# Turning tokens into features: 32x32 transposes on VectorE in place of 128x128 ones on TensorE, in one decoder block

## The chip, the cores and the metric

The kernel runs on one core of a Trainium2 chip. The metric is the device time of one execution in microseconds; where several executions were made, the median stands for them. A separate, profiled execution gives the trace; its own time is given beside its span.

## What is computed

One layer of a hybrid decoder on 256 tokens of 2048 features, all in fp32:

```python
h = rmsnorm(x, norm_mix_g)
c_g, b_g, xa, za, q, fl, iv, og, ga, gb = split(h @ w_in)
ya = b_g * causal_dwconv3(c_g * xa, conv_w) * silu(za)
# log_f and kk come from sigmoid(fl), sigmoid(-fl)
o = hgrn2_chunked(silu(q), kk, iv, log_f)          # gated linear recurrence, 8 heads of 128
yb = rmsnorm_per_head(o) * hg_norm_g * silu(og)
m = sigmoid(ga) * (ya @ w_a_out) + sigmoid(gb) * (yb @ w_b_out)
x = x + m @ w_o
x = x + sigmoid(rmsnorm(x, ple_norm_g) @ w_ple_gate) * (p @ w_ple_proj)
out = rmsnorm(x, final_norm_g)
```

Every product has the activations' features on the contracted axis. A product leaves tokens on the partitions (two tiles of 128 tokens) and 512 features along the free axis; whatever goes into a further product, into the convolution along the tokens or into the recurrence must have features on the partitions. So blocks of 256 tokens x 512 features are turned from tokens to features: one *turn* in the sense of this text.

## The kernel before

**Groups and steps.** The work is a list of groups, each one block of 512 output columns: for column block j = 0 and 1 the groups f, q, iv, og, c, xa, za, b; then for j = 0 to 3 the groups ga, gb, A (ya times w_a), B (yb times w_b); then four groups O (m times w_o); then PP and PG for each of four blocks. A group is cut into steps along the contracted axis, 256 features each: eight steps for most groups, four for A and B, one for PP. In this text steps are counted from zero over the whole kernel: f is 0 to 7, q 8 to 15, iv 16 to 23, og 24 to 31, c 32 to 39, xa 40 to 47, za 48 to 55, b 56 to 63, and then the same for j = 1.

**A step.** The weights arrive in fp32 by one SP queue into `raw` (three buffers, two steps each). For precision each weight block is split in two parts: ScalarE writes the high part `whi` (L118) and VectorE the rest `wlo` = raw - whi (L119). Activations are split the same way by `put` (L154 and L155). TensorE then does twelve matmuls for a step: two blocks of 128 features, two token tiles, and three products each, high by high (L805), high activations by `wlo` (L806), low activations by `whi` (L807). Splits are written three steps ahead of use, and there are four buffers of each part, so `whi` of step n+3 can be written when TensorE has finished step n-1.

**Epilogues.** When a group's last step is written, a generator for it is started; after each later step, `advance()` runs every active generator up to its next `yield`. So the work behind a group is spread over the following steps, between the splits. The written order is what the framework starts from; it then draws up the order on each engine, and an instruction that is ready early may go ahead of others.

**The turns.** Before, `transposed` (L170 to L184) does eight 128x128 transposes on TensorE against an identity, into two banks of the PSUM tag `s`, and a reader takes the result from PSUM. `ep_o` has the same in its own lines (L576). The eighteen turns are:

- f (two): L218, read by four sigmoids on ScalarE (L223, L224). A chain of scalings, logarithms (L244) and a scan (L253) follows.
- q (two): L270, copied to SBUF by VectorE (L274).
- yb, the output of the recurrence (two): L456, read by `put`.
- xa (two): L474, read by the convolution, four heads of one L487 and seven L493 on VectorE.
- b (two): L512, multiplied with the convolution on VectorE (L517), then split (L520, L521).
- B (four): L551, split on ScalarE and VectorE (L556, L557) into `mT`.
- O (four): L576, read by `put` into `x1T`.

Beside them in the same steps runs `hgrn`, the recurrence (L292 to L461), started after og: level by level differences and products on VectorE and GpSimd (L355, L338), small products on TensorE (L310), masked copies on VectorE (L314), a reciprocal (L400), and at its end a sum of squares (L443) and eight products (L450) that make yb. The tail of xa's convolution and the middle of `hgrn` meet in steps 48 to 58, and b's turn and the end of `hgrn` meet in steps 64 to 69.

Scratch tiles come from `t4`, eight buffers of 128x1024 in the first part and five in the later ones.

Of the kernel before, what the change touches and what calls it, by code (L numbers as in the profile page):

```python
# [9 lines left out]

F32 = mybir.dt.float32
F32R = mybir.dt.float32r
AF = mybir.ActivationFunctionType
ALU = mybir.AluOpType
# [31 lines left out]
def hybrid_kernel(ctx, tc, xT, x, pT, prm, gfin, masks, w_in, w_a, w_b, w_o, w_pg, w_pp, out):  # L46
# [35 lines left out]
    def bank(tag):  # L82
        return ps.tile([P, CW], F32, tag=tag, bufs=4, name=nm(tag))
# [39 lines left out]

    prm_t = const.tile([P, PRM_N], F32, name="prm_t")
    nc.scalar.dma_start(out=prm_t, in_=prm)
    ident = const.tile([P, P], F32, name="ident")
    make_identity(nc, ident)

    if PAD_CONST:
        nc.gpsimd.memset(const.tile([P, PAD_CONST], F32, name="pad"), 0.0)  # L130
# [36 lines left out]
        nc.gpsimd.tensor_tensor(out=r, in0=v, in1=mhalf[:, :n], op=ALU.pow)  # L167
        return r

    def transposed(src):  # L170

        banks = []
        for half in range(2):
            b = bank("s")
            for i in range(2):
                c = half * 2 + i
                for t in range(NT):
                    nc.tensor.transpose(  # L178
                        b[:, i * T + t * P : i * T + (t + 1) * P],
                        src[:, t * CW + c * P : t * CW + (c + 1) * P],  # L180
                        ident,
                    )
            banks.append(b)
        return banks  # L184


    def scaled(psum, dst):
# [26 lines left out]
    def ep_f(j, psum):  # L214
        fl = t4()
        scaled(psum, fl)
        yield
        bk = transposed(fl)  # L218
        yield
        sg, sn = t4(), t4()  # L220
        for h in range(2):
            s = slice(h * 512, (h + 1) * 512)
            nc.scalar.activation(out=sg[:, s], in_=bk[h], func=AF.Sigmoid)  # L223
            nc.scalar.activation(out=sn[:, s], in_=bk[h], func=AF.Sigmoid, scale=-1.0)  # L224
        yield
        kT = t4("kT", 1)
        for h in range(4):
            s = slice(h * T, (h + 1) * T)
            hd = j * 4 + h
            nc.vector.tensor_scalar(  # L230
                out=sg[:, s], in0=sg[:, s], scalar1=state["oml"][:, hd : hd + 1],
                scalar2=state["lbm"][:, hd : hd + 1], op0=ALU.mult, op1=ALU.add,
            )
            nc.vector.tensor_scalar(
                out=kT[:, s], in0=sn[:, s], scalar1=state["oml"][:, hd : hd + 1], scalar2=None,
                op0=ALU.mult,
            )
        yield


        lf, last = t4(), sc(8, "lfl", 2)
        lv, fv = segments(lf), segments(sg)
        nc.gpsimd.memset(lv[:, :, 1, :, 0:1], 0.0)
        nc.scalar.activation(out=lv[:, :, 0], in_=fv[:, :, 0], func=AF.Ln)  # L244
        nc.scalar.activation(
            out=lv[:, :, 1, :, 1:], in_=fv[:, :, 1, :, : SCAN - 1], func=AF.Ln
        )
        nc.scalar.activation(
            out=last.rearrange("p (h s) -> p h s", h=4), in_=fv[:, :, 1, :, SCAN - 1], func=AF.Ln
        )  # L250
        yield
        b, tot = t4("b", 1), sc(16, "tot", 2)
        nc.vector.tensor_tensor_scan(  # L253
            out=b, data0=carry, data1=lf, initial=0.0, op0=ALU.mult, op1=ALU.add
        )
        bv, tv = segments(b), tot.rearrange("p (h k s) -> p h k s", h=4, k=2)
        nc.vector.tensor_copy(out=tv[:, :, 0], in_=bv[:, :, 0, :, SCAN - 1])
        nc.vector.tensor_tensor(
            out=tv[:, :, 1], in0=bv[:, :, 1, :, SCAN - 1],
            in1=last.rearrange("p (h s) -> p h s", h=4), op=ALU.add,  # L260
        )
        state["kT", j], state["b", j], state["tot", j] = kT, b, tot

    def ep_q(j, psum):
        sg, qt = t4(), t4()
        sig(psum, sg)
        times(psum, sg, qt)
        yield
        yield
        bk = transposed(qt)  # L270
        yield
        qT = t4("qT", 1)
        for h in range(2):
            nc.vector.tensor_copy(out=qT[:, h * 512 : (h + 1) * 512], in_=bk[h])  # L274
        state["qT", j] = qT

    def ep_iv(j, psum):
# [14 lines left out]
    def hgrn(j):  # L292
# [159 lines left out]
                op0=ALU.mult, op1=ALU.mult,  # L452
            )
        yield
        yield
        bk = transposed(yb)  # L456
        yield
        for h in range(2):
            for i in range(2):
                k = j * 4 + h * 2 + i  # L460
                put(state["ybT"], k, bk[h][:, i * T : (i + 1) * T], gain(PRM_GHG, k))  # L461

    def ep_c(j, psum):
        c = t4()
# [4 lines left out]
    def ep_xa(j, psum):  # L469
        cx = t4()  # L470
        times(psum, state["c", j], cx)
        yield
        yield
        bk = transposed(cx)  # L474
        yield
        cv = t4("cv", 1)
        for h in range(2):
            for i in range(2):
                n = h * 2 + i
                k = j * 4 + n  # L480
                d, s = cv[:, n * T : (n + 1) * T], bk[h][:, i * T : (i + 1) * T]

                def w(tap):
                    c = PRM_CONV + tap * 8 + k
                    return prm_t[:, c : c + 1]

                nc.vector.tensor_scalar(out=d, in0=s, scalar1=w(2), scalar2=None, op0=ALU.mult)  # L487

                for tap, to, fr, n_ in (
                    (1, 1, 0, P - 1), (1, P, P + 1, P - 1), (1, T - 1, P - 1, 1),  # L490
                    (0, 2, 0, P - 2), (0, P, P + 2, P - 2), (0, T - 2, P - 1, 1), (0, T - 1, P - 2, 1),
                ):
                    nc.vector.scalar_tensor_tensor(  # L493
                        out=d[:, to : to + n_], in0=s[:, fr : fr + n_], scalar=w(tap), in1=d[:, to : to + n_],
                        op0=ALU.mult, op1=ALU.add,
                    )
            yield
        state["cv", j] = cv
# [8 lines left out]
    def ep_b(j, psum):  # L507
        bz = t4()
        times(psum, state["zs", j], bz)
        yield  # L510
        yield
        bk = transposed(bz)  # L512
        yield
        ya = t4()
        for h in range(2):
            s = slice(h * 512, (h + 1) * 512)
            nc.vector.tensor_tensor(out=ya[:, s], in0=state["cv", j][:, s], in1=bk[h], op=ALU.mult)  # L517
        yield
        hi, lo = (x[:, j * 4 : (j + 1) * 4, :].rearrange("p k t -> p (k t)") for x in state["yaT"])
        nc.scalar.activation(out=hi, in_=ya, func=AF.Copy)  # L520
        nc.vector.tensor_tensor(out=lo, in0=ya, in1=hi.bitcast(F32), op=ALU.subtract)  # L521
# [21 lines left out]
    def ep_bb(j, psum):  # L543
        ga, gb = state["ga", j], state["gb", j]
        for t in range(NT):
            s = slice(t * CW, (t + 1) * CW)
            nc.vector.tensor_tensor(out=gb[:, s], in0=gb[:, s], in1=psum[t], op=ALU.mult)  # L547
        nc.gpsimd.tensor_tensor(out=gb, in0=ga, in1=gb, op=ALU.add)  # L548
        yield
        yield  # L550
        bk = transposed(gb)  # L551
        yield
        for h in range(2):
            k = j * 4 + h * 2
            hi, lo = (x[:, k : k + 2, :].rearrange("p k t -> p (k t)") for x in state["mT"])
            nc.scalar.activation(out=hi, in_=bk[h], func=AF.Copy)  # L556
            nc.vector.tensor_tensor(out=lo, in0=bk[h], in1=hi.bitcast(F32), op=ALU.subtract)  # L557

    def ep_o(j, psum):
        xs = state["x"]  # L560
        src = t4()
        for t in range(NT):
            d = xs[:, t, j * CW : (j + 1) * CW]
            nc.vector.tensor_tensor(out=d, in0=d, in1=psum[t], op=ALU.add)
            nc.scalar.activation(
                out=src[:, t * CW : (t + 1) * CW], in_=d, func=AF.Square,
                accum_out=state["ss2"][:, t * 4 + j : t * 4 + j + 1],
            )
        yield
        bk = []  # L570
        for half in range(2):
            b = bank("s")
            for i in range(2):
                c = j * 4 + half * 2 + i
                for t in range(NT):
                    nc.tensor.transpose(  # L576
                        b[:, i * T + t * P : i * T + (t + 1) * P], xs[:, t, c * P : (c + 1) * P], ident
                    )
            bk.append(b)
        yield  # L580
        for h in range(2):
            for i in range(2):
                k = j * 4 + h * 2 + i
                put(state["x1T"], k, bk[h][:, i * T : (i + 1) * T], gain(PRM_GPLE, k))
        if j == 3:
            tot = sc(2, "tot2", 1)
            nc.vector.tensor_reduce(
                out=tot, in_=state["ss2"].rearrange("p (t j) -> p t j", t=NT),
                axis=mybir.AxisListType.X, op=ALU.add,
            )  # L590
            state["rstd2"] = rsqrt_of(tot, NT, D, "r2")
# [369 lines left out]
```

## Time and profile before

| | us |
|---|---|
| median of three executions | 852.69 (852.5 to 853.07) |
| the profiled execution's own time | 852.66 |
| its span | 850.9 |
| TensorE's eight-transpose groups, L178 and L576, durations summed | 10.6 + 4.1 + 4.1 |
| wlo L119 on VectorE, all | 372.6 |
| whi L118 on ScalarE, all | 308.6 |

The profile lists each engine's busy time, the chain of work that ended last (followed back from the last instruction through what released each step), groups of instructions by source line with the mean duration of one, the waits between engines, and a timeline. In the names, PE is TensorE, PEld its weight load, DVE is VectorE, ACT is ScalarE, POOL is GpSimd, and SP the queue that issues transfers. Matmuls are pipelined, so a row's duration is longer than the distance to the next row, and it is the distance that adds up. In the waits, "A <- B" means that A stood idle until B released it; the three numbers are the total, the count and the longest, in us. In the rows of groups, the numbers behind the bar are busy us in all, mean ns of one, and the idle time just before. A bracket in the timeline gives the idle time before that row and what ended it; a row without one began at once. TensorE's granted clock is 0.998 of full speed over the span.

### The profile page before, as it was taken

What the parts mean: (1) busy time and instruction counts of PE and PEld (TensorE: products, weight loads), DVE (VectorE), ACT (ScalarE), POOL (GpSimd) and SP (SyncE); (2) the same over time, 40 slices, a digit from 0 to 9 for tenths busy, and PEclk for the clock granted to TensorE, in tenths of its full rate; (3) what the DMA queues carried; (4) which work ended last, traced back from release to release, by engine and by line L of the source; (5) the groups of instructions that cost most, each with busy time, mean ns of one, the idle gap of its engine ahead of it and who ended that gap; (6) DMA issues with size and microseconds to landing.
All of it is one profiled execution on the core that took longest, in us unless ns stands there. A gap on an engine that the chain in (4) does not pass through costs nothing.

```text
span 850.9 us, 9907 instructions
## 1 busy us (share of the span) xinstructions
PE 839.6 (99%) x3897; PEld 697.8 (82%) x3897; DVE 527.2 (62%) x611; ACT 425.0 (50%) x514; POOL 82.8 (10%) x76
## 2 busy tenths in 40 slices
PE   9999999999999999999999999999999999999995
PEld 6788888888888888888888888888888888888885
DVE  7484686977674587968446446446446555556572
ACT  7854664434644754534443444444444554455553
POOL 1010042202010042101001001001001000001110
PEclk9999999999999999999999999999999999999999
DMA  9865464444555455444555555555555955554542
GB/s 340 335 215 184 158 223 162 171 174 155 191 199 177 169 198 178 169 165 174 169 191 191 198 197 199 171 193 188 190 198 173 362 181 186 184 196 165 197 149 99
DMA packets 25966, 164.12 MB, mean 193 GB/s; under 512 B 3008, under 2 KB 3008, under 8 KB 7744
## 3 DMA queue, kind: packets, MB, share of 16 engines
q1 hardware_dynamic: 25488, 162.93, 53.8%
q8 instruction: 30, 0.49, 0.2%
q10 hardware_dynamic: 432, 0.56, 0.2%
q14 instruction: 16, 0.13, 0.0%
HBM read 161.39 MB, written 2.10 MB: 192 GB/s over the span
## 4 chain that ended last, share of the span: by engine, by line
PE 96%; issue 1%; DMA 1%; ACT 1%; DVE 0%; SPq 0%; POOLq 0%; POOL 0%; ACTq 0%
PE g L806 31%; PE g L807 31%; PE g L805 31%; PE s L310 1%; PE s L178 1%; DMA raw<-in_w_in 1%; PE s L418 0%; PE s L576 0%; PE s L430 0%; PE s L431 0%; PE s L429 0%; ACT whi L118 0%; ACT xs L647 0%; ACT t L630 0%; SPq L700 0%
## 5 line engine op out<-in xcount | busy, mean ns | idle before, releaser
L119 DVE TENSOR_TENSOR wlo<-raw,whi 128x1024 fp32r<-128x1024 f32 (+1 forms) x294 | 372.6, 1273 | 270.6 <-ACT whi L118 270.0
L118 ACT ACTIVATE whi<-raw 128x1024 fp32r<-128x1024 f32 (+1 forms) x294 | 308.6, 1053 | 361.9 <-PE g L807 354.4
L805 PE MATMUL g<-whi,xh 128*128 128x512 f32 (+1 forms) x912 | 354.5, 389 | 0.9 <-ACT whi L118 0.9
L806 PE MATMUL g<-wlo,xh 128*128 128x512 f32 (+1 forms) x912 | 352.0, 386 | 0.2 <-DVE wlo L119 0.2
L807 PE MATMUL g<-whi,xl 128*128 128x512 f32 (+1 forms) x912 | 351.8, 386 | 0.0
L805 PEld LDWEIGHTS g<-whi,xh 128*128 128x128 f32 x912 | 171.5, 188 | 35.5 <-ACT whi L118 2.3
L806 PEld LDWEIGHTS g<-wlo,xh 128*128 128x128 f32 x912 | 171.5, 188 | 34.8 <-DVE wlo L119 1.2
L807 PEld LDWEIGHTS g<-whi,xl 128*128 128x128 f32 x912 | 171.4, 188 | 34.4
L805 PE MATMUL g<-whi,mh 128*128 128x512 f32 x128 | 50.2, 392 | 0.0
L807 PE MATMUL g<-whi,ml 128*128 128x512 f32 x128 | 49.9, 390 | 0.0
L806 PE MATMUL g<-wlo,mh 128*128 128x512 f32 x128 | 49.8, 389 | 0.0
L548 POOL TENSOR_TENSOR gb<-ga,gb 128x1024 f32<-128x1024 f32 x4 | 9.6, 2396 | 258.3 <-DVE gb L547 258.3
L807 PEld LDWEIGHTS g<-whi,ml 128*128 128x128 f32 x128 | 24.0, 188 | 5.1
L806 PEld LDWEIGHTS g<-wlo,mh 128*128 128x128 f32 x128 | 24.0, 188 | 4.9
L805 PEld LDWEIGHTS g<-whi,mh 128*128 128x128 f32 x128 | 24.0, 188 | 4.8
L338 POOL TENSOR_TENSOR X<-t,kT 128x256 f32<-128x256 f32 x12 | 11.5, 956 | 168.3 <-ACT t L352 115.4
L805 PE MATMUL g<-whi,yaTh 128*128 128x512 f32 x64 | 24.9, 389 | 0.0
L806 PE MATMUL g<-wlo,yaTh 128*128 128x512 f32 x64 | 24.9, 389 | 0.0
L807 PE MATMUL g<-whi,yaTl 128*128 128x512 f32 x64 | 24.9, 389 | 0.0
L805 PE MATMUL g<-whi,ybTh 128*128 128x512 f32 x64 | 24.9, 389 | 0.0
L806 PE MATMUL g<-wlo,ybTh 128*128 128x512 f32 x64 | 24.9, 389 | 0.0
L807 PE MATMUL g<-whi,ybTl 128*128 128x512 f32 x64 | 24.9, 389 | 0.0
(153 smaller groups left out, 559.1 us busy)
## 6 DMA issues: line engine op xcount, KB each, us to landing
raw<-in_w_in SPq DMA_DIRECT2D x91, 1024.0 KB, 4.8
raw<-in_w_o SPq DMA_DIRECT2D x16, 1024.0 KB, 4.8
raw<-in_w_pg SPq DMA_DIRECT2D x16, 1024.0 KB, 4.7
raw<-in_w_a SPq DMA_DIRECT2D x8, 1024.0 KB, 5.0
raw<-in_w_b SPq DMA_DIRECT2D x8, 1024.0 KB, 5.0
raw<-in_w_in SPq DMA_DIRECT2D x9, 512.0 KB, 7.8
t<-in_xT SPq DMA_DIRECT2D x8, 256.0 KB, 7.0
t<-in_x SPq DMA_DIRECT2D x4, 512.0 KB, 8.7
```

The source lines that it names most:

```text
L118: nc.scalar.activation(out=hi[:, s], in_=src[:, s], func=AF.Copy)
L119: nc.vector.tensor_tensor(out=lo[:, s], in0=src[:, s], in1=hi[:, s].bitcast(F32), op=ALU.subtract)
L178: nc.tensor.transpose(b[:, i * T + t * P : i * T + (t + 1) * P], src[:, t * CW + c * P : t * CW + (c + 1) * P], ident,)
L310: nc.tensor.matmul(bk[:, s], X[:, 0, h, :], X[:, 1, h, :], start=True, stop=True)
L338: eng.tensor_tensor(out=xv[:, w, :, :, half, :], in0=ev[:, :, blk, :, half, :], in1=src[:, :, blk, :, half, :], op=ALU.mult,)
L548: nc.gpsimd.tensor_tensor(out=gb, in0=ga, in1=gb, op=ALU.add)
L805: nc.tensor.matmul(psum, oh, hi, start=first, stop=False)
L806: nc.tensor.matmul(psum, oh, lo, start=False, stop=False)
L807: nc.tensor.matmul(psum, ol, hi, start=False, stop=last)
```

## The change

All eighteen turns move to VectorE. `transposed`, its TensorE transposes and the identity go. A new generator `turned` does a turn by sixteen `nc.vector.transpose` calls: each takes one quarter of the partitions (32) of the source with every fourth 32-column piece, eight 32x32 blocks in all (32 partitions x 256 elements), and writes them, each block transposed, to a quarter of the partitions of the result in SBUF. The quarter read changes with every call, the quarter written with every fourth. It yields after every `step` calls: four per step in most turns, eight in yb and in the last O.

```diff
-    def transposed(src):
-        banks = []
-        for half in range(2):
-            b = bank("s")
-            ...
-                    nc.tensor.transpose(
-            ...
+    def turned(src, dst, step):
+        s = src.rearrange("p t (c b e) -> p t c b e", b=4, e=32)
+        d = dst.rearrange("p c (t a e) -> p t c a e", t=NT, e=32)
+        for n in range(16):
+            a, b = n % 4, n // 4
+            nc.vector.transpose(
+                out=d[32 * b : 32 * b + 32, :, :, a, :], in_=s[32 * a : 32 * a + 32, :, :, b, :]
+            )
+            if n % step == step - 1:
+                yield
```

The users change with it. The result is a `t4` tile in SBUF, and readers read that in place of PSUM. Two examples, f and b:

```diff
-        bk = transposed(fl)
-        yield
-        sg, sn = t4(), t4()
-        for h in range(2):
-            s = slice(h * 512, (h + 1) * 512)
-            nc.scalar.activation(out=sg[:, s], in_=bk[h], func=AF.Sigmoid)
-            nc.scalar.activation(out=sn[:, s], in_=bk[h], func=AF.Sigmoid, scale=-1.0)
+        sn = t4()
+        yield from turned(by_tile(fl), by_feature(sn), 4)
+        sg = t4()
+        nc.scalar.activation(out=sg, in_=sn, func=AF.Sigmoid)
+        nc.scalar.activation(out=sn, in_=sn, func=AF.Sigmoid, scale=-1.0)
...
-        yield
-        bk = transposed(bz)
-        yield
         ya = t4()
-        for h in range(2):
-            s = slice(h * 512, (h + 1) * 512)
-            nc.vector.tensor_tensor(out=ya[:, s], in0=state["cv", j][:, s], in1=bk[h], op=ALU.mult)
+        yield from turned(by_tile(bz), by_feature(ya), 4)
+        nc.vector.tensor_tensor(out=ya, in0=state["cv", j], in1=ya, op=ALU.mult)
```

In q the turn writes `qT` itself, so the copy L274 goes. In xa, yb and O a new `t4` tile (`cxT`, `yT`, `x1`) holds the result; the convolution and `put` read it. In B a new tile `m` holds it, and the split becomes one instruction of 1024 columns on each engine. Where a turn stood between two empty yields before, its first four (or eight) transposes now come one step after the product that they turn, and the reader comes four steps (two in yb and the last O) after that.

More of the change, by code (lines that the diff above doesn't have):

```diff
@@ L8 @@
 from concourse._compat import with_exitstack
-from concourse.masks import make_identity
 F32 = mybir.dt.float32
@@ L125, in hybrid_kernel @@
     nc.scalar.dma_start(out=prm_t, in_=prm)
-    ident = const.tile([P, P], F32, name="ident")
-    make_identity(nc, ident)
     if PAD_CONST:
@@ L168, in rsqrt_of, with by_tile, by_feature @@
         return r
-    def transposed(src):
-        banks = []
-        for half in range(2):
-            b = bank("s")
[L175 to L184, printed above, removed]
+    def by_tile(ap):
+        return ap.rearrange("p (t n) -> p t n", t=NT)
+    def by_feature(ap):
+        return ap.rearrange("p (c n) -> p c n", n=T)
+    def turned(src, dst, step):
[8 more added lines that the diff above has]
+                yield
     def scaled(psum, dst):
@@ L268, in ep_q @@
         yield
-        yield
-        bk = transposed(qt)
-        yield
         qT = t4("qT", 1)
-        for h in range(2):
-            nc.vector.tensor_copy(out=qT[:, h * 512 : (h + 1) * 512], in_=bk[h])
+        yield from turned(by_tile(qt), by_feature(qT), 4)
         state["qT", j] = qT
@@ L454, in hgrn @@
         yield
[L455 to L461, printed above, removed]
+        yT = t4()
+        yield from turned(by_tile(yb), by_feature(yT), 8)
+        for c in range(4):
+            k = j * 4 + c
+            put(state["ybT"], k, yT[:, c * T : (c + 1) * T], gain(PRM_GHG, k))
     def ep_c(j, psum):
@@ L472, in ep_xa @@
         yield
-        yield
-        bk = transposed(cx)
-        yield
+        cxT = t4()
+        yield from turned(by_tile(cx), by_feature(cxT), 4)
         cv = t4("cv", 1)
@@ L480, in ep_xa @@
                 k = j * 4 + n
-                d, s = cv[:, n * T : (n + 1) * T], bk[h][:, i * T : (i + 1) * T]
+                d, s = cv[:, n * T : (n + 1) * T], cxT[:, n * T : (n + 1) * T]
                 def w(tap):
@@ L510, in ep_b @@
         yield
-        yield
-        bk = transposed(bz)
-        yield
         ya = t4()
-        for h in range(2):
-            s = slice(h * 512, (h + 1) * 512)
-            nc.vector.tensor_tensor(out=ya[:, s], in0=state["cv", j][:, s], in1=bk[h], op=ALU.mult)
+        yield from turned(by_tile(bz), by_feature(ya), 4)
+        nc.vector.tensor_tensor(out=ya, in0=state["cv", j], in1=ya, op=ALU.mult)
         yield
@@ L549, in ep_bb @@
         yield
[L550 to L557, printed above, removed]
+        m = t4()
+        yield from turned(
+            gb.rearrange("p (t n) -> p t n", t=NT), m.rearrange("p (c n) -> p c n", c=4), 4
+        )
+        k = j * 4
+        hi, lo = (x[:, k : k + 4, :].rearrange("p k t -> p (k t)") for x in state["mT"])
+        nc.scalar.activation(out=hi, in_=m, func=AF.Copy)
+        nc.vector.tensor_tensor(out=lo, in0=m, in1=hi.bitcast(F32), op=ALU.subtract)
     def ep_o(j, psum):
@@ L569, in ep_o @@
         yield
[L570 to L584, printed above, removed]
+        x1 = t4()
+        yield from turned(xs[:, :, j * CW : (j + 1) * CW], x1.rearrange("p (c n) -> p c n", c=4), 8 if j == 3 else 4)
+        for c in range(4):
+            put(state["x1T"], j * 4 + c, x1[:, c * T : (c + 1) * T], gain(PRM_GPLE, j * 4 + c))
         if j == 3:
```

## Prediction

> **What bounds the kernel now.** I read the page's engine sums and its chain first, then who waits for whom, then the timeline of TensorE and VectorE around the turns.
>
> ```profile
> PE 839.6 (99%) x3897; PEld 697.8 (82%) x3897; DVE 527.2 (62%) x611; ACT 425.0 (50%) x514; POOL 82.8 (10%) x76
> ...
> PE 96%; issue 1%; DMA 1%; ACT 1%; DVE 0%; SPq 0%; POOLq 0%; POOL 0%; ACTq 0%
> ```
> TensorE is 96% of the chain that ends last, and VectorE is busy 62% of the span. The waits say why the two do not disturb each other:
>
> ```profile
> ACT whi L118 <- PE g L807: 354.4, 217, 3.5
> DVE wlo L119 <- ACT whi L118: 270.0, 203, 3.2
> ```
> ScalarE waits for TensorE to hand back a weight buffer, VectorE waits for ScalarE, and nobody of size waits for VectorE. The low half of the weights is early. How early is read from the timeline: in the steady stretches the wlo of step n ends 5.6 us before the first matmul of step n. That is the cover under which VectorE may be late.
>
> **What goes.** A step is twelve matmuls. TensorE's timeline around the turn of B, column block 0:
>
> ```profile
> 455.80 0.39 PE L807 MATMUL g<-whi,xl 128*128 128x512 f32 x1
> ...
> 458.52 0.40 PE L807 MATMUL g<-whi,xl 128*128 128x512 f32 x1
> 458.76 1.04 PE L178 MATMUL s<-ident,gb 128*128 128x128 f32 x8
> ...
> 462.17 0.39 PE L807 MATMUL g<-whi,xl 128*128 128x512 f32 x1
> ```
> From the first to the second line are twelve matmuls, 458.52 - 455.80 = 2.72 us. From the second to the last are twelve more with eight transposes between, 3.65 us. A turn costs TensorE 3.65 - 2.72 = 0.93 us, not the sum of the eight rows' durations. Seventeen turns stand in such places: 17 x 0.93 = 15.8. The first, f0 at 29 to 32 us, stands where TensorE waits for wlo 8 anyway (six of its transposes run from 31.10, wlo 8 ends at 31.58, the next matmul is at 31.82): 0.24. **Gain at most 16.05 us**: 852.66 - 16.05 = 836.6 if nothing takes its place. Also gone: four copies L274 (0.69 each) and the identity on GpSimd, both off the chain. ScalarE's four sigmoids of 0.6 per f become two of about 1.06, no worse.
>
> **What comes.** 18 x 16 = 288 transposes on VectorE, each of 32 partitions x 256 elements. The trace of before has none. Rows of 256 fp32 elements from SBUF are the nearest:
>
> ```profile
> L408 DVE TENSOR_TENSOR kT<-kT,t 128x256 f32<-128x256 f32 x4 | 1.7, 416 | 0.0
> L234 DVE TENSOR_SCALAR kT<-t,lc 128x256 f32<-128x256 f32 x8 | 2.7, 346 | 0.0
> L338 DVE TENSOR_TENSOR X<-t,qT 128x256 f32<-128x256 f32 x12 | 11.0, 919 | 0.0
> ```
> Rows that follow one another start sooner than they last: L408 is followed 0.34 after its start, L234 by 0.26, a wlo of 1.23 by 1.14. So the low end is 0.26 a transpose. The high end is 0.92, the slowest row of this size. I take 0.42, the duration of L408, with no overlap: every overlap seen is between instructions on all 128 partitions, and each transpose goes to other partitions than the one before. The instruction behind a run of four loses its 0.08 too, so four cost 4 x 0.42 + 0.08 = 1.76.
>
> [...]
>
> On average all this fits: 288 x 0.42 = 121 us, VectorE at 648 of about 850. But it has to fit stretch by stretch. VectorE has 2.72 - 1.15 = 1.57 us a step beside the wlo; a step with four transposes is 0.19 over, 0.8 in four steps, under a cover of 5.6. So B (4), O (4; the last with eight a step: 1.3 of sums and two steps of 1.15 + 3.52 put its wlo 1.4 to 2 us ahead of use), f and q (4) are covered. The mT of the last B is wanted two steps after the subtraction that makes it; I count it done 1 to 2 us before. The raw buffers come back as wlo's finish: 5.6 us later, a load of 4.8 still lands 0.6 before it is wanted, so that is next to be late.
>
> **Stretch one: xa, twice.** Here VectorE has no idle time (no brackets) from 148 to 179 us:
>
> ```profile
> 166.13 1.20 DVE L119 TENSOR_TENSOR wlo<-raw,whi 128x1024 fp32r<-128x1024 f32 x1
> 167.26 3.34 DVE L400 RECIPROCAL t<-t 128x512 f32<-128x512 f32 x1
> 170.52 1.15 DVE L119 TENSOR_TENSOR wlo<-raw,whi 128x1024 fp32r<-128x1024 f32 x1
> ```
> The last of these is the wlo of step 58; it ends at 171.67 and step 58 starts at 175.80: 4.1 us of cover. The conv, the level products and the reciprocal are written before it, and the sixteen transposes too. With TensorE 0.93 earlier the cover is 3.2. VectorE ends 16 x 0.44 = 7.0 later, less some 0.4 because the conv reads SBUF in place of PSUM (0.41 against 0.47 in L230 and L487). Stall: 7.0 - 0.4 - 3.2 = **3.4 us**.
>
> **Stretch two: b and yb, twice.** b turns in steps 64 to 67 (four a step), yb in 66 and 67 (eight a step).
>
> ```profile
> 196.71 1.40 DVE L205 SCALAR_TENSOR_TENSOR t<-g,r1r,t 128x512 f32<-128x512 f32 x2
> ...
> 206.31 1.22 DVE L521 TENSOR_TENSOR yaTl<-t,yaTh 128x1024 fp32r<-128x1024 f32 x1 [1.13 <-ACT yaTh L520]
> 207.46 1.22 DVE L119 TENSOR_TENSOR wlo<-raw,whi 128x1024 fp32r<-128x1024 f32 x1
> 209.79 1.23 DVE L119 TENSOR_TENSOR wlo<-raw,whi 128x1024 fp32r<-128x1024 f32 x1 [1.11 <-ACT whi L118]
> ```
> There is some idle time, but 32 transposes (14.1 us) come within four steps. VectorE's queue in the order written, from the start of step 64 (196.62) as zero: L205 to 1.4; wlo 67 to 2.55; four to 4.3; wlo 68 to 5.45; eight L450 at 0.26 to 7.55; four to 9.3; wlo 69 to 10.45; twelve (5.28) to 15.75; wlo 70 to 16.9, wanted at 6 x 2.72 = 16.3: 0.6 late. Twelve more to 22.2, wlo 71 to 23.35, wanted at 19.6: 3.7 late. The four puts (1.6), the product with cv (1.15) and wlo 72 to 27.25, wanted at 26.05: 1.2 late. Then steps with little else let it catch up. Stall: 0.6 + 3.7 + 1.2 = **5.5 us**. ScalarE, in order, stands behind the same transposes with the puts' high halves; it is free at about 25, when wlo 72 is due to start.
>
> **Sum**: 852.66 - 16.05 + 2 x (3.4 + 5.5) = 854.4, called **854.5**. The profiled 852.66 (span 850.9) and the median 852.69 are one number here.
>
> **Rivals.** First, *overlap holds* between transposes: 0.34 each, none lost behind. Stretch one stalls 1.8, stretch two 2.3 (wlo 70 in time, 71 late by 1.1, 72 by 1.2); 852.66 - 16.05 + 8.2 = 844.8, faster. The turning point between faster and slower lies near 0.40 a transpose (both stretches then stall 8.0). For it: every back-to-back pair in the trace overlaps. Against: all those pairs keep their partitions.
> Second, *the order spares the weights*: the instruction order on an engine is not simply the written one (L383 is written for step 54 and runs at 149.74, before the wlo written for step 49). If wlo's pass the transposes, all are covered: 836.6. Against: between 154 and 172 the order is nearly the written one, and transposes, which wait for nothing, leave no gap to pass in.
> Third, *a transpose is dear*: 0.68, as a row of 512 elements (L355), if fp32 goes through in two halves. Stretches 7.6 and 13.8, twice, 43 us, and the last O with f and q some 10: about 889.
> Fourth, *it doesn't do what it says*: one call becomes several instructions. Eight of 0.13 (the spacing of the 128x1 rows of L493) are 1.04 a call, 300 us on VectorE, which then bounds at 880 to 950.
>
> **Chances.** Forecast 0.48 (850 to 860), overlap 0.2, order 0.1, dear 0.13, several 0.04, and 0.05 for what I don't see. The forecast's mass lies across the edge of what a measurement of this kernel tells from no change, 0.2% or 1.7 us: 0.03 of it below, 0.16 within, 0.29 above. Faster 0.34 with the two rivals; same 0.16; slower 0.5. Range 838 to 872: from just above the full gain (0.26 a transpose gives 837.7) to 0.58 a transpose (stretches 6.0 and 10.6, twice, 2 elsewhere: 872). The end at 0.92 lies far outside and is left with the 2 in 10; the forecast's own range is 850 to 860.
>
> **What will show it.** The transposes' rows: 288 of them, duration near 0.42 and spacing equal to it. TensorE's waits for wlo L119, now 1.4 us, should grow to some 18, in four places: near 175, 211, and the same of column block 1 near 365 and 400; nowhere else. Steps at the turns of B and O should be 2.72. If TensorE's waits lie on ScalarE's whi or on raw loads, the hand-on was mis-seen; if the stalls stand elsewhere, the order was; if spacing is 0.34 or under, the first rival has it.

## The result and the profile after

| | before | after |
|---|---|---|
| median of four executions, us | 852.66 (852.5 to 853.07) | 866.33 (865.74 to 869.4) |
| profiled execution, its span | 852.66, 850.9 | 865.74, 863.9 |
| ratio with 95% interval | | 1.0167 [1.0142, 1.0191] |

The change makes the kernel 13.7 us slower. The forecast was 854.5, so its sign held and the result lies in the range of 838 to 872, but the sum is 11.8 us short and the result lies outside the forecast's own 850 to 860. The executions of the kernel after that took longer also show a lower mean granted clock (869.4 at 0.984, 865.74 at 0.991).

The engine sums and the shares of the chain that ended last, of the kernel after:

```profile
PE 832.1 (96%) x3753; PEld 685.0 (79%) x3753; DVE 646.3 (75%) x889; ACT 423.2 (49%) x506; POOL 84.0 (10%) x74
...
PE 74%; DVE 18%; issue 4%; ACT 2%; DMA 1%; POOL 0%; SPq 0%; POOLq 0%; ACTq 0%; DVEq 0%
```

TensorE has 144 instructions fewer and stays at 96% of a longer span. By the sums VectorE has a quarter of its time to spare; by the chain it sets the end for 18% of the span, where it set 0% before. Both are true, of different stretches. The waits of the kernel after:

```profile
ACT whi L117 <- PE g L786: 304.7, 184, 4.9
DVE wlo L118 <- ACT whi L117: 160.0, 127, 3.3
...
PEld g L785 <- DVE wlo L118: 17.7, 17, 3.9
...
PE g L785 <- DVE wlo L118: 10.8, 8, 3.5
...
PE s L307 <- DVE X L388: 6.1, 2, 3.1
```

The first two are the healthy waits of before, and both shrank: VectorE waited 270.0 us for ScalarE and now 160.0. The next two are the new thing: TensorE and its weight load stand for wlo (with 96% and 79% of the span the two overlap in time, so their waits do not add up). The last line counts as much: TensorE's small products in the recurrence wait for VectorE's X, 6.1 us in two waits.

**Where the 13 us are.** I took the start of each step of the kernel before and after, and charged each stretch of steps with what the span grew in it plus 0.93 for each turn that left it (0.24 for the first f):

| steps | turns | loss, us | forecast |
|---|---|---|---|
| 0 to 48 | f, q of block 0 | 1.8 | 0 |
| 48 to 62 | xa of block 0 | 5.2 | 3.4 |
| 62 to 76 | b and yb of block 0, f of block 1 | 6.4 | 5.5 |
| 76 to 112 | q of block 1 | 2.8 | 0 |
| 112 to 126 | xa of block 1 | 5.0 | 3.4 |
| 126 to 140 | b and yb of block 1 | 6.2 | 5.5 |
| 140 to 228 | four B | 0.0 | 0 |
| 228 to 232 | the last B's mT is late for O | 1.4 | 0 |
| 232 to the end | four O | 0.4 | 0 |

Before rounding the losses sum to 29.1 us; the gain is the 16.05 of the prediction, and 29.1 - 16.05 is the difference of the two spans, 13.0, but for rounding.

**The price.** One group of transposes of the kernel after:

```profile
L183 DVE STREAM_TRANSPOSE t<-t 32x256 f32<-32x256 f32 x128 | 55.7, 435 | 2.1
```

435 ns each. In a run they start 0.449 us apart, so none starts before the end of the one before. The first starts only when the wlo before it has ended (1.26 from its start, where other instructions follow after 1.14), the instruction behind the last starts 0.47 after it. So four add 3 x 0.449 + 0.469 + 0.12 = 1.93 us to VectorE.

**Stretch one.** The timeline of VectorE in the kernel after (a row that ends in xN spans N instructions):

```profile
160.17 1.79 DVE L183 STREAM_TRANSPOSE t<-t 32x256 f32<-32x256 f32 x4
...
163.74 1.65 DVE L481 TENSOR_SCALAR cv<-t,prm_t 128x256 f32<-128x256 f32 x2
...
173.33 1.23 DVE L118 TENSOR_TENSOR wlo<-raw,whi 128x1024 fp32r<-128x1024 f32 x1
174.47 0.69 DVE L388 TENSOR_TENSOR X<-t,kT 128x512 f32<-128x512 f32 x1
```

and of TensorE:

```profile
171.86 0.39 PE L786 MATMUL g<-whi,xl 128*128 128x512 f32 x1
175.31 2.04 PE L307 MATMUL s<-X 128*128 128x128 f32 x8 [3.06 <-DVE X L388]
176.99 0.77 PE L784 MATMUL g<-whi,xh 128*128 128x512 f32 x1
177.57 0.63 PE L785 MATMUL g<-wlo,xh 128*128 128x512 f32 x1
...
178.80 0.40 PE L785 MATMUL g<-wlo,xh 128*128 128x512 f32 x1
```

The forecast had the wlo of step 58 late. What is late first is X, the operand of the last product at L307 in the recurrence: L388 ends at 175.16, and TensorE stands 3.45 us between starts before those eight products (171.86 to 175.31). The same stretch of block 1 has two waits on TensorE, and the wlo of its step 122, which corresponds to step 58, is not one of them:

```profile
PE s L307 <- DVE X L388: 3.1, 1, 3.1
...
PE s L415 <- DVE kT L405: 1.1, 1, 1.1
```

Both are for operands of the recurrence. The reader should also see the rows behind the stall of block 0: matmuls 0.42 apart instead of 0.23. The profile's windows, with the columns us, busy time of the five engines, granted clock, DMA share and GB/s, after the two stalls of block 0 and after the stall of block 1 that has the same length as the first:

```profile
175.35:178.75 3.40, 3.40 (x12) 3.11 (x13) 3.40 (x3) 2.92 (x4) 1.63 (x2) 0.50 0.89 308
226.55:229.90 3.35, 3.35 (x10) 2.57 (x9) 3.35 (x5) 1.07 (x2) 0.00 (x0) 0.50 0.83 306
374.60:378.00 3.40, 3.40 (x19) 2.98 (x20) 3.40 (x3) 2.91 (x4) 1.65 (x2) 1.00 0.88 308
```

The granted clock is 0.50 for 3.41 us behind the first two (and from 424.5), and 1.00 behind the third.

**Stretch two**, VectorE's timeline in the kernel after:

```profile
211.08 1.23 DVE L118 TENSOR_TENSOR wlo<-raw,whi 128x1024 fp32r<-128x1024 f32 x1
212.22 5.36 DVE L183 STREAM_TRANSPOSE t<-t 32x256 f32<-32x256 f32 x12
217.61 1.23 DVE L118 TENSOR_TENSOR wlo<-raw,whi 128x1024 fp32r<-128x1024 f32 x1
218.87 5.42 DVE L183 STREAM_TRANSPOSE t<-t 32x256 f32<-32x256 f32 x12
224.32 1.23 DVE L118 TENSOR_TENSOR wlo<-raw,whi 128x1024 fp32r<-128x1024 f32 x1
```

and TensorE's:

```profile
225.60 0.50 PE L785 MATMUL g<-wlo,xh 128*128 128x512 f32 x1 [3.47 <-DVE wlo L118]
```

This is the queue that the prediction wrote down, twelve, wlo 70, twelve, wlo 71; it had wlo 71 late by 3.7 and TensorE waits 3.47.

### The profile page after: what moved, and what is told of

Its sections match the earlier page's. It is cut to its first block, busy times and chain, and to the rows that moved or that the text cites. A ratio compares the mean times of both kernels' runs of the same rounds, so it can differ in the third digit from the quotient of the medians.

```text
span 863.9 us, 9867 instructions
## 1 busy us (share of the span) xinstructions
PE 832.1 (96%) x3753; PEld 685.0 (79%) x3753; DVE 646.3 (75%) x889; ACT 423.2 (49%) x506; POOL 84.0 (10%) x74
## 4 chain that ended last, share of the span: by engine, by line
PE 74%; DVE 18%; issue 4%; ACT 2%; DMA 1%; POOL 0%; SPq 0%; POOLq 0%; ACTq 0%; DVEq 0%
PE g L785 24%; PE g L786 24%; PE g L784 24%; DVE t L183 6%; DVE wlo L118 6%; ACT whi L117 1%; DVE cv L487 1%; DVE qT L183 1%; PE s L307 1%; DMA raw<-in_w_in 1%; DVE t L208 1%; DVE X L335 0%; DVE cv L481 0%; PE s L415 0%; DVE t L397 0%
## 5 line engine op out<-in xcount | busy, mean ns | idle before, releaser
L785 PE MATMUL g<-wlo,xh 128*128 128x512 f32 (+1 forms) x912 | 355.0, 389 | 11.1 <-DVE wlo L118 10.8
L785 PEld LDWEIGHTS g<-wlo,xh 128*128 128x128 f32 x912 | 172.6, 189 | 51.6 <-DVE wlo L118 17.7
L183 DVE STREAM_TRANSPOSE t<-t 32x256 f32<-32x256 f32 x128 | 55.7, 435 | 2.1
L785 PE MATMUL g<-wlo,mh 128*128 128x512 f32 x128 | 49.8, 389 | 0.0
L538 POOL TENSOR_TENSOR gb<-ga,gb 128x1024 f32<-128x1024 f32 x4 | 9.6, 2398 | 259.8 <-DVE gb L537 259.8
L183 DVE STREAM_TRANSPOSE t<-xs 32x256 f32<-32x256 f32 x64 | 27.9, 436 | 1.1
L183 DVE STREAM_TRANSPOSE t<-gb 32x256 f32<-32x256 f32 x64 | 27.9, 435 | 1.0
L785 PEld LDWEIGHTS g<-wlo,mh 128*128 128x128 f32 x128 | 24.0, 188 | 5.0
L785 PE MATMUL g<-wlo,yaTh 128*128 128x512 f32 x64 | 24.9, 389 | 0.0
```

Of the source, the lines that this page charges most:

```text
L183: nc.vector.transpose(out=d[32 * b : 32 * b + 32, :, :, a, :], in_=s[32 * a : 32 * a + 32, :, :, b, :])
L785: nc.tensor.matmul(psum, oh, lo, start=False, stop=False)
```

## The experiments

All kernels start from the kernel after; where a turn goes back to TensorE, it is done as before. Ratios are to the kernel before, measured again each time, with the 95% interval. A diff block that gives only a number of transposes per step, or a description in words, sums the edit up and is not code. T1 in the expectations is the theory that VectorE is short of time in the stretches of xa and of b with yb, T2 the rivals named there.

**Which turns cost.** Four kernels divide the change. With the four B and four O alone on VectorE (shown for xa; f, q, b and yb likewise):

```diff
-        yield from turned(by_tile(cx), by_feature(cxT), 4)
+        yield
+        bk = transposed(cx)
+        yield
...
```

> Only the eight turns of B and O go to VectorE, the other ten stay on TensorE. Theory 1 (the time is lost in a few stretches, where the transposes stand in the same steps as much other VectorE work): eight turns at 0.93 us are saved, and only the last B hands over mT late, 1.4 us in the changed kernel's trace: 852.7 - 7.4 + 1.4 = 846.6. Theory 2 (every transpose costs alike, through VectorE's total load: the changed kernel lost 13.7 + 16.05 = 29.7 us to 288 of them, 0.103 each): 128 of them, 852.7 - 7.4 + 13.2 = 858.4.

Measured: 847.32, ratio 0.9936 [0.9922, 0.9951]. With xa alone on VectorE (shown for b; f, q, yb, B and O likewise):

```diff
-        yield from turned(by_tile(bz), by_feature(ya), 4)
+        yield
+        bk = transposed(bz)
+        yield
...
```

> Only the two turns of xa go to VectorE. Theory 1: the stretch at the end of the convolution loses what it lost in the changed kernel, 5.2 and 5.0 us, two turns saved: 852.7 + 10.1 - 1.9 = 860.9, with TensorE standing before the product L307 of the recurrence and then at half the granted clock for a short time. Theory 2 (alike): 32 transposes, 852.7 + 3.3 - 1.9 = 854.1.

Measured: 861.25, 1.0100 [1.0085, 1.0115]. With b and yb alone on VectorE (xa goes back to TensorE in place of b and yb, by the same edit):

> Only the turns of b and yb, four, go to VectorE. Theory 1: 6.4 and 6.2 us lost as in the changed kernel, four turns saved: 852.7 + 12.6 - 3.7 = 861.6, with TensorE's wait for wlo at the fourth step after the two turns begin. Theory 2 (alike): 64 transposes, 852.7 + 6.6 - 3.7 = 855.6.

Measured: 861.81, 1.0115 [1.0099, 1.0132]. With f, q, B and O on VectorE, and xa, b and yb on TensorE:

> All turns but xa, b and yb go to VectorE: f, q, B, O, twelve of eighteen. Theory 1: to the 846.6 of B and O alone come four turns saved less what the changed kernel lost around f and q (2.8 us in steps 82 to 87, 1.8 in the first 24, half a turn less saved at the first f): 846.6 - 3.0 + 4.6 = 848.2. Theory 2 (alike): 192 transposes, 852.7 - 10.5 + 19.8 = 862.0.

Measured: 846.58, 0.9930 [0.9915, 0.9945]. All four answer for T1; its sum for the last was 1.6 us too high. The two turns of xa cost 8.5 us and the four of b and yb 9.0; the other twelve gain 6.2. The parts add up to +11.2 against the +13.7 of the whole. Most of the difference is q of block 1: its stretch loses 2.8 us in the whole change and 0.65 here, where VectorE comes out of the stretch before without the backlog of b and yb.

TensorE's waits in the kernel with xa alone, and in the one with b and yb alone (other line numbers, the same lines of code as L307 and L785):

```profile
PE s L346 <- DVE X L427: 6.1, 2, 3.1
```

```profile
PEld g L858 <- DVE wlo L119: 11.3, 7, 3.9
...
PE g L858 <- DVE wlo L119: 8.4, 5, 3.5
```

The two long stalls of the whole change are there alone, at their full length. The mean granted clock of the two profiled executions is 0.993 and 0.994, for 0.998 before.

**Is it the lumps or the sum?** All turns on VectorE, thinner:

```diff
-    f, q, xa, b: turned(..., 4); yb: turned(..., 8)
+    f, q, xa, b: turned(..., 2); yb: turned(..., 4)
-    last B: turned(..., 4)
+    last B: turned(..., 8)
```

> All eighteen turns on VectorE, the same 288 transposes, only spread thinner: two a step in f, q, xa and b, four in yb; B four, but the last B eight a step so that mT is handed over earlier; O as in the change. Theory 1 (piling up in a few steps): two transposes are 0.9 + 0.1 us beside a wlo of 1.15 in a step of 2.72, the full gain of 16.05 comes through but for some 2 us: about 838 to 841. Theory 2 (alike, by number of transposes): 866. A third view, that the order drawn up by the framework falls anyhow in the crowded stretches: 850 to 860.

Measured: 850.98, 0.9979 [0.9970, 0.9989]. This is far from the 838 to 841 of theory 1 and within the third view. 15 of the 29 us come back and the rest moves: about 2 us at each of steps 61 and 125, 0.5 to 1 at 56, 74, 120 and 138, 1.8 at 86 to 89, 1.5 at 8 and 1.7 at 236. So the lumps are half of it. A part of the other half is a sum. From 200 to 275 us VectorE was busy for 47.5 us before; 64 transposes at about 0.48 make 30.7, in all 78 of 75. The window of the thinner kernel:

```profile
200.00:275.00 75.00, 73.61 (x317) 58.58 (x316) 73.25 (x120) 37.52 (x44) 3.61 (x4) 1.00 0.49 169
```

VectorE (the third sum) is busy 73.25 of 75. TensorE did 317 matmul rows there, 292 with the change as it is; the 348 of before include 32 transposes, so the thinner kernel does hardly more products in this time than the kernel before, and what the four turns freed is lost. Steps 62 to 112, which this window covers, make 3.6 of the 14.3 us that are still lost. For the rest the sum is not shown: from 140 to 196 us VectorE was busy for 44.66 us before, sixteen transposes at 0.48 make it 52.3 of 56, which fits, and yet steps 56 and 61 lose 2.6. VectorE has no idle time from 168 to 193 us there; what fills that shorter stretch was not worked out. The same with only xa, b and yb made thinner:

```diff
-    xa, b: turned(..., 4); yb: turned(..., 8)
+    xa, b: turned(..., 2); yb: turned(..., 4)
```

> The change with only xa and b at two transposes a step and yb at four, all else as in the change. Theory 1: the 10.1 us of xa and most of the 12.6 of b and yb come back, some 1 to 3 remain: 844 to 848. Theory 2: 866, since the number of transposes is the same.

Measured: 855.03, 1.0029 [1.0017, 1.0040], between the two, against my expectation: losses at 61 and 125 (2 each), 74 to 79 and 83 (2.6).

**Is it one operand that comes too late?** If X is what TensorE waits for, making X earlier should help. With xa alone on VectorE, X for the last product is written four steps earlier:

```diff
     for i, level in enumerate(LEVELS):
         ...
+        if i == len(LEVELS) - 2:
+            last_X = products of X[:, 0] and X[:, 1]
-    e = t4() ... X[:, 0], X[:, 1]
```

> As e2 (xa alone on VectorE, 861.25), with the recurrence's last product's operand X (L380, L388 in the change, nothing else) written four steps earlier, before the convolution's second half. Same work on every engine. If the stall of xa is one late operand, L307 waiting for X behind the convolution, it goes: what stays late is the wlo of step 58, by about 0.5 us in each block: 852.7 - 1.9 + 2 = 853 (852 to 855), and no half-clock windows. If the stall is the sum of VectorE's work in the stretch, as the prediction had it, some 3.4 each stay: 857 to 860.

Measured: 862.04, 1.0109 [1.0095, 1.0123], no better than 861.25, and also above the 857 to 860 of the sum. My theory of one operand fell. The waits of this kernel:

```profile
PE s L456 <- DVE kT L446: 4.5, 2, 2.3
PEld g L871 <- DVE wlo L119: 4.3, 5, 1.4
```

The wait for X is gone, and TensorE waits for kT and for a wlo further on, with a granted clock of 0.53 behind the wait for kT (181.95 to 185.30). Which operand is late depends on the order. That one is late fits the sum of VectorE's work: from 148 to 182 us VectorE is busy for 33.62 of 34 us in both kernels. Neither expectation has a term for the half clock, which follows twice here (0.53 again from 376.45 to 379.80).

**Why do transposes not overlap?** For B alone, each transpose is cut in two that read and write the same partitions:

```diff
-            nc.vector.transpose(out=d[32*b:32*b+32, :, :, a, :], in_=s[32*a:32*a+32, :, :, b, :])
+            for t in range(NT):
+                nc.vector.transpose(out=d[32*b:32*b+32, t, :, a, :], in_=s[32*a:32*a+32, t, :, b, :])
```

> Only the four turns of B on VectorE, and each transpose is cut into two of 128 elements that stand one behind the other with the same quarter of the partitions read and the same written. Theory H (an instruction on another quarter of the partitions waits until the one before has finished): duration near 0.435 - 0.133 = 0.30; the second of a pair starts before the first ends, spacing 0.21 to 0.23; the first of the next pair only after the end, spacing 0.31. Theory N (transposes never overlap): spacing 0.31 in both places. The time itself, 32 instead of 16 instructions a turn, near 849 to 851.

Two rows of VectorE's timeline, each of a window so narrow that the row spans two instructions:

```profile
461.96 0.49 DVE L189 STREAM_TRANSPOSE t<-gb 32x128 f32<-32x128 f32 x2
462.19 0.57 DVE L189 STREAM_TRANSPOSE t<-gb 32x128 f32<-32x128 f32 x2
```

The first row is the two halves of one transpose (nine halves stand before the wlo ahead of these rows, so the one behind it ends a pair and the next begins one). The second row is a second half with the first of the next pair. Halves that come first last 0.30, those that come second 0.26. Within a pair they take 0.49, which is 0.07 less than the sum of the two; across pairs 0.57, which is 0.01 more. So what is lost is the overlap, and it is lost where the partitions change. In starts, a half begins 0.23 after the first of its pair and 0.27 after the second of the pair before. That is theory H, with second halves of 0.26 in place of its 0.30. No row was named for the 0.133 of its expectation; rows of before give the same: 128x512 lasts 0.684 (L355), 128x256 0.416 (L408), so 128 elements fewer are 0.134 less. The time of this kernel, 854.39 in its only execution, missed its 849 to 851: the last B is later still, and TensorE loses 2.7 us at steps 229 and 230 and 2.2 at 233, where the first turn of O waits for xs.

**What is the best mix?** With f, q, B and O on VectorE and the last B at eight a step:

```diff
-    last B: turned(..., 4)
+    last B: turned(..., 8)
```

> f, q, B and O on VectorE as in the run before with twelve turns (846.6), but the last B turned with eight transposes a step. If the 1.4 us lost at steps 229 and 230 come from mT being asked for two steps after it is split: 845.2, and no wait for ml or mh. If eight a step push the wlo past use instead: 846.6 to 848, with waits for wlo near 660.

Measured: 849.44, 0.9962 [0.9949, 0.9974], worse than 846.58 and than both of its expectations. The wait for mT is gone, but the transposes of O follow nearly in a row behind a 2.9-us wait of VectorE for a load of xs, and the wlo of step 236 is 3.0 late. Two kernels add one turn to f, q, B and O: yb at four a step, or b at two:

```diff
-    yb: transposes on TensorE
+    yb: turned(..., 4)
```

```diff
-    b: transposes on TensorE
+    b: turned(..., 2)
```

> f, q, B and O on VectorE as in e4, and yb too, at four transposes a step; xa and b on TensorE. Theory S (a stretch's own sum decides: what VectorE does in it before, plus 16 x 0.48 us a turn, against its length): from 200 to 275 us VectorE is busy 47.7 us before; with f, q and yb 47.7 + 23 = 71 of 75, so it fits and two turns more are saved: 846.6 - 1.9 = 844.7, up to 846 if the order costs something. Theory A (each transpose costs alike, what e1 to e4 already speak against): 850.

> As the run before, but b instead of yb goes to VectorE, at two transposes a step. Theory S: the same sum, 71 of 75: 844.7 to 846. If instead the place in the queue matters more than the sum, b's longer turn meets f's of the next block (the last of its transposes come with f1's first) and it loses 2 to 3: 847 to 848.

Measured: 845.38, 0.9919 [0.9905, 0.9933], and 845.40, 0.9919 [0.9906, 0.9933]. In the first, VectorE's sum from 200 to 275 is 67.3 of 75 and TensorE is busy for 74.5 of them: one more turn a block fits, and two, in the thinner kernels, did not. It is not free: q of block 1 behind it loses 1.8 us instead of 0.65. Last, f, q, yb, O, three B and the second b on VectorE, xa, the first b and the last B on TensorE:

```diff
-    xa: turned(..., 4); b of block 0: turned(..., 4); last B: turned(..., 4)
+    xa, b of block 0, last B: transposes on TensorE
-    yb: turned(..., 8); b of block 1: turned(..., 4)
+    yb: turned(..., 4); b of block 1: turned(..., 2)
```

> The version that the runs point to: f, q, yb, O and the first three B on VectorE, of b only the second block's (two a step, yb four a step); xa, the first b and the last B stay on TensorE. By the stretch's sum: after the second block's b VectorE was busy 20.1 of 38 us (392 to 430) and 32 transposes bring 15.4, 35.5 of 38, so it fits with up to 1 us lost; against e9 (845.4) one turn of b is saved (0.93), the last B costs its 0.93 again and the 1.4 us of late mT go: 844.0, and 844 to 845.4. If another stretch takes the loss over, as e5 and e7 had it: 846 or more.

Measured: 845.74, 0.9917 [0.9903, 0.9930], the same as the two before within their intervals and 0.3 above its 844 to 845.4. The stall of the last B is gone as expected; 1.1 us are lost at the second b, and the first 48 steps lose 2.4 where they lose 1.55 with yb alone added, with a granted clock of 0.54 from 32.0 to 35.4 there (see the last section). The best of the change is thus about 845.4 us, 0.8% under the kernel before, with the turns of xa and one of b and yb left on TensorE.

## Why the prediction was right and where it failed

The sign and the range held, the forecast's own 850 to 860 did not. That the result lies in the range is partly luck: its upper end stood for a transpose of 0.58 us, and the transposes came near the forecast's price; losses that the sum did not have fill the room.

- **The gain.** 0.93 us for each turn holds: steps at the turns of B and O last 2.72 in the kernel after, as said. Twelve turns moved alone save 10.5 and lose 4.0, 1.4 of it at the last B.
- **The price.** 0.42 and 1.76 for four were said, 0.435 with 0.449 from start to start and 1.93 were measured. There is one row per call, 288 in all. This ends three rivals: that transposes overlap (0.34), that one is dear (0.68), and that a call becomes several instructions. The fourth, that VectorE's order spares the weights, ended too: the wlo's stand between the runs of transposes, late.
- **Stretch two** was right in mechanism and place. In size, 11.0 was said and 12.6 measured (with f of block 1 in it), and a part of this nearness is chance. In block 0 step 70 loses 1.0 for the 0.6 said, TensorE stands 3.5 at step 71 for the 3.7 said, and the 1.2 at wlo 72 did not come; the half clock behind the stall, which the sum did not have, adds some 1.6 in each block.
- **Stretch one** was right in place and mis-sized: 6.8 said, 10.1 measured. The step that failed is "the last of these is the wlo of step 58": I measured the cover on one consumer of VectorE's queue. X and kT, which TensorE wants in the same steps, were in the same queue, with less cover; in block 1 the stalls at X and kT make nearly the whole 5.0. That X alone is not the cause is shown by the run that moved it. VectorE's work was mis-sized too. The sixteen transposes cost 4 x 1.93 = 7.7 for the 7.0 said. The convolution's rows, from start to start, take 7.8 for 7.2 before, where 0.4 less was said: the two L481 at 163.74 take 1.65 for 0.87 before, beside a product of GpSimd (L389, 1.49 from 163.49). Together that is 1.7 more for VectorE, about what each stretch lost beyond the 3.4 said.
- **"So B, O, f and q are covered"** failed for f and q and for the last B, 5.9 us where nothing was said. The cover of 5.6 us is that of the steady stretches; q of block 1 comes when VectorE still carries the backlog of b and yb (2.8, against 0.65 in the kernel without them), and f and q of block 0 come near the start (1.8). The mT of the last B was counted 1 to 2 us in time and is 1.4 late. VectorE's wlo ahead of that turn lasts 3.33 instead of 1.23 while GpSimd's 2.40-us addition (L538) runs; the same slow wlo was in the trace of before, and the sum left it out. That it makes the difference was not tested alone.
- **The clock** had no term. In the three half-clock windows twenty matmuls are 0.2 apart more than at full clock, and the eight products at 175.31 take 1.68 until the next matmul where the same eight at 374.57 take 0.88: 4.0 + 0.8 = 4.8 us, contained in the losses of the table. In stretch one it did not come on top: block 0 loses 5.2 with a half-clock window, and block 1 loses 5.0 without one, where TensorE stands for kT instead.
- **The signs.** TensorE's waits for wlo were to grow to some 18 us near 175, 211 and the same of block 1, and nowhere else. They grew to 10.8 (17.7 at the weight load), in stretch two as said; in stretch one the waits are for X and kT, and some stand at q of block 1 (1.2 between 255 and 275) and near the start, where none was expected.

The profiled execution is 11.2 us over the forecast (the median another 0.6): 5.9 are cases called covered, 3.3 stretch one, 1.6 stretch two and 0.4 the end. The 4.8 us of the clock are part of what stretches one and two lost.

## What to carry to other kernels

An engine that is busy 62% of the span is not free 38% of each stretch: add the new work to its busy time stretch by stretch, carry the excess into the next one, and look at every consumer of its queue, not only the one that waits today. Move the turns whose stretch has room and leave the others: fourteen of these eighteen turns are worth 0.8%, all of them cost 1.7%. A stall of TensorE may cost some 1.6 us again in clock, as three of the four stalls of over 3 us here did, so it can be worth more to avoid than its length.

## What the runs showed of the hardware

In the kernel after, half the clock was granted in three windows, from 175.3, 226.5 and 424.5, for 3.41 us each. Each follows a stall of TensorE of over 3 us. The first and the third begin where the stall ends (the products start at 175.31, L785 at 424.49), the second 0.9 us later (L785 starts at 225.60). The stall at 371 to 374.5 has none behind it (1.00 from 374.60 to 378.00), though it is as long as the first one (3.06 us in both). Nor does it take 3 us: in the last kernel of the experiments the granted clock is 0.54 from 32.00 to 35.40, behind two start-up waits of 1.10 and 0.53 us; the same two waits in the kernel with yb added have no half clock behind them. The window of the two kernels in turn:

```profile
32.00:35.40 3.40, 3.40 (x9) 2.62 (x10) 3.28 (x7) 2.08 (x3) 0.00 (x0) 0.54 0.70 239
```

```profile
32.00:35.40 3.40, 3.40 (x16) 2.77 (x17) 3.28 (x7) 1.94 (x3) 0.00 (x0) 1.00 0.70 249
```

Nine matmul rows against sixteen, for the same instructions at this place and the same waits before them. The matmuls ahead of it stand alike too: the last before the first wait starts at 29.23 in the one and at 29.08 in the other, the first behind it at 30.72 and 30.57, the first behind the second wait at 31.98 and 31.83. In the kernel after the three are 29.29, 30.78 and 32.04, with the same waits of 1.10 and 0.53, and the matmuls behind them are 0.23 apart, with a granted clock of 1.00 from 32.0 to 35.4. So stalls of the same length came with half the clock behind them and without it; what decides was not shown.
